# Weight and feature remainders on VectorE in place of GpSimd, in a hybrid diffusion layer

## Chip, core and metric

The kernel runs on one core of a Trainium2 chip. The metric is the device time of one execution in microseconds (us). Engines are named as the profile names them: PE is TensorE's matmul, PEld its weight load, DVE is VectorE, ACT is ScalarE, POOL is GpSimd, and SP is SyncE, which issues most DMAs. Each engine works off its own instructions strictly in their order, and waits on semaphores for what other engines and DMAs produce.

## The reference, cut to what matters

One layer of a backbone runs over 128 context tokens and 1024 latent tokens, with a width of 1024. In the kernel's order:

```python
h  = rmsnorm(x, norm1_w) * (1 + sc1) + sh1          # adaLN modulation
aq, ak, av, mq, mk, mv, mo, mg = split(h @ w_in)    # 2832 columns
attn_o = attention(aq, [ak, cached], [av, cached])  # 8 query heads, 2 key heads, 64 wide
hm     = bidirectional mLSTM(mq, mk, mv, gates)     # 4 heads, 128 wide, chunks of 128
x  = x + g1 * (concat(attn_o, hm * sigmoid(mo)) @ w_out)
h2 = rmsnorm(x, norm2_w) * (1 + sc2) + sh2
g, u = split(h2 @ w_gu)                             # 2 x 2816 columns
x  = x + g2 * ((silu(g) * u) @ w_down)
y  = rmsnorm(x, final_norm_w)
```

Everything is float32 outside, and the kernel keeps that accuracy. It splits an operand into an upper half, rounded to the type that the matmul reads (fp32r, or float16), and a lower half, the remainder `full - hi`. A product is then three matmuls: upper by upper, upper by lower, lower by upper. The lower halves are what this change is about.

## The kernel before, in words

The tokens stand in nine blocks of 128, and these in three chunks of 384 (`CB` = 3 blocks).

The work has these stages. First come the modulation vectors from `w_ada`, the norm of x, and `features(c)`, which makes the modulated features of a chunk as float16 pairs `hTh` and `hTl`. For each of eight column groups it writes the upper half on ACT and the full value on DVE, and subtracts (line 137, `sub`). The groups with an even number subtract on DVE, the others on POOL. Then the projections by `w_in` run: keys, values and gates, then q, then four mLSTM heads. Their weights are `Scaled` objects of four tiles each. `pairs()` makes float16 pairs of them. With its default `dve_every=2`, tiles 0 and 2 are done by one ACT instruction and one fused DVE instruction (line 222), and tiles 1 and 3 by two on ACT and a `sub` on POOL (line 226, shown as line 137). The pairs of keys, values and gates use `dve_every=1` and so the fused form alone. Attention and the mLSTM scans run woven between these matmuls.

`attn_out_first` and `prefill` apply `w_out`, and `norm2` makes the input of the FFN. Then the three FFN chunks follow (`gate_up`, `down`, `down_last`). A chunk works through 22 blocks of the FFN's width in five groups. For each block `gate_up` loads a piece of the gate columns and one of the up columns and runs 24 matmuls of 384 columns for each piece (lines 1315 to 1317). The activation follows: tanh on ACT (line 1333), two instructions on DVE into the tile tn (1334 and 1335), its upper half hl on ACT (1338), its lower half on POOL (also line 137, `hl<-tn,hl`, not touched by the change). After a group's four or five blocks `down` multiplies by `w_down` (lines 1115 to 1117) and adds into x on DVE (`add_gated`, lines 1104 and 1105). During the first two chunks the attention of the next chunk is woven in: scores S on PE (1035), row maximum st on DVE (1037), exp on ACT (1038), upper part ph on ACT (1041), lower part pl on DVE (1042), then two transposing DMAs and the products by the values (1059, 1060). S has one buffer.

All float32 weights, 216 pieces of `w_out`, `w_gu` and `w_down` in the buffers named raw, whi and wlo and a few more in borrowed buffers (`ir`, `ip`), go through `load_piece`. SP loads 512 KB into raw (two buffers), ACT copies it rounded into whi (line 154), and `sub` writes `raw - whi` to wlo (line 137). whi and wlo have five buffers each, so a piece can be prepared while PE works on earlier ones; a raw buffer is free again once its subtraction is done. A count decides the engine: every third piece subtracts on DVE, the two others on POOL.

The source gives priorities (`hot`) and interleavings (`weave`, `beside`). The final order of each engine's instructions is laid out ahead of time by the planner of the framework, which plays the program through with its own costs (`schedule_with_timeline_sim`). A change of an instruction's engine therefore changes the order that it plans.

Of the kernel before, what the change touches and what calls it, by code (L numbers as in the profile page):

```python
# [8 lines left out]
F32 = mybir.dt.float32  # L9
# [36 lines left out]
def hybrid_step(ctx: ExitStack, tc: tile.TileContext, I: dict, O: dict):  # L46
# [3 lines left out]
    dve = nc.vector  # L50
    pool = nc.gpsimd
# [6 lines left out]
    def nm(s):  # L58
        uid[0] += 1
        return f"{s}_{uid[0]}"  # L60
# [75 lines left out]
    def sub(out, full, hi, eng):  # L136
        (dve if eng == "dve" else pool).tensor_tensor(out=out, in0=full, in1=hi, op=ALU.subtract)  # L137

    lo_count = [0]

    def load_piece(srcs, shape, dve_every=3, raw=None, own=None):

        a, b = shape
        n = a * b

        def view(t):
            return t[:, :n].rearrange("p (a b) -> p a b", b=b)

        raw = raw or wp.tile([P, 1024], F32, name=nm("raw"), tag="raw", bufs=2)
        hi = own[0] if own else wp.tile([P, 1024], F32R, name=nm("whi"), tag="whi", bufs=5)  # L150
        lo = own[1] if own else wp.tile([P, 1024], F32R, name=nm("wlo"), tag="wlo", bufs=5)
        for part, ap_ in srcs:
            dma(part(view(raw)), ap_)
        nc.scalar.copy(hi[:, :n], raw[:, :n])  # L154
        lo_count[0] += 1
        sub(lo[:, :n], raw[:, :n], hi[:, :n].bitcast(F32), "dve" if lo_count[0] % dve_every == 0 else "pool")
        return view(hi), view(lo)

    full_view = lambda v: v
# [22 lines left out]
    class Scaled:  # L182
# [31 lines left out]
        def pairs(self, dve_every=2):  # L214
            out = []
            n, b = self.n, self.shape[1]
            for j, raw in enumerate(self.raws):
                w = wp.tile([P, 2, 1024], F16, name=nm("ipair"), tag="ipair", bufs=4)
                hi, lo = w[:, 0, :n], w[:, 1, :n]
                if j % dve_every == 0:  # L220
                    act(hi, raw[:, :n], AF.Copy, scale=self.scale)
                    dve.scalar_tensor_tensor(out=lo, in0=raw[:, :n], scalar=self.scale, in1=hi, op0=ALU.mult, op1=ALU.subtract)  # L222
                else:
                    act(raw[:, :n], raw[:, :n], AF.Copy, scale=self.scale)
                    nc.scalar.copy(hi, raw[:, :n])
                    sub(lo, raw[:, :n], hi, "pool")
                out.append(tuple(v.rearrange("p (a b) -> p a b", b=b) for v in (hi, lo)))
            return out

# [271 lines left out]
    def features(c):  # L501

        v = x3[c].rearrange("p b (k x) -> p k b x", k=KD)
        hh, hl = (t[c].rearrange("p k (b x) -> p k b x", b=CB) for t in (hTh, hTl))
        for k in range(KD):
            full = p0.tile([P, CB, P], F32, name=nm("full"), tag="full", bufs=4)
            for i, n in ((0, 1), (1, 2)) if c == 0 else ((0, CB),):
                cnd = 0 if n == 1 else 1
                s, t = scale1[:, k, cnd : cnd + 1], shift1[:, k, cnd : cnd + 1]
                act(hh[:, k, i : i + n], v[:, k, i : i + n], AF.Identity, scale=s, bias=t)  # L510
                dve.tensor_scalar(out=full[:, i : i + n], in0=v[:, k, i : i + n], scalar1=s, scalar2=t, op0=ALU.mult, op1=ALU.add)
            sub(hl[:, k], full, hh[:, k], "dve" if k % 2 == 0 else "pool")

    for c in range(NCH):
        with hot(100):
            features(c)
        prods = linear_tok(kvg_pairs, 0, 272, evac_kvg, (tuple(range(c * CB, c * CB + CB)),), bank if c == 1 else bankA)
        if c > 0:
            weave(prods, chain(steps, ada), KD, 10)
        else:  # L520
            emit(prods)
        if c == 0:
            normalise(2)
        if c == 1:
            turn(2)
# [597 lines left out]
    def out_pieces(half, own=None):  # L1123
        ws = []
        for n in range(2):
            pieces = []
            for j in range(2):
                r0 = half * 512 + 2 * j * P
                rows = w_out[r0 : r0 + 2 * P, n * 512 : (n + 1) * 512].rearrange("(a p) n -> p a n", p=P)
                pieces.append(load_piece([(full_view, rows)], (2, 512), raw=own and own[2], own=own))  # L1130
                own = None
            ws.append(pieces)
        return ws
# [74 lines left out]
    def attn_out_first(oT, ready):  # L1208
# [16 lines left out]
        def out():  # L1225
            for n in range(2):
                cs = slice(n * 512, (n + 1) * 512)
                ws = []
                for j in range(2):
                    rows = w_out[2 * j * P : (2 * j + 2) * P, cs].rearrange("(a p) n -> p a n", p=P)  # L1230
                    ws.append(load_piece([(full_view, rows)], (2, 512), raw=ir[2], own=(ip[j], ir[j])))
                for cnd in range(2):
                    dma(gt[:, 2 * n + cnd], g_d[0, cnd : cnd + 1, cs].to_broadcast([P, 512]))
                yield
                for i in range(CB):
                    while i not in ready:
                        yield
                    th, tl = mx[:, i, 0:4], mx[:, i, 4:8]
                    if n == 0:
                        dma(x1[:, i], xrow(i))  # L1240
                        nc.scalar.copy(th, oT[i])
                        sub(tl, oT[i], th.bitcast(F32), "pool")
                        yield
                    ps = out_block([ws], 0, th, tl)
                    v = x1[:, i, cs]
                    dve.tensor_tensor(out=gt[:, 4], in0=ps, in1=gt[:, 2 * n + (i > 0)], op=ALU.mult)
                    pool.tensor_tensor(out=v, in0=v, in1=gt[:, 4], op=ALU.add)
                    yield
                    if n == 1:
                        dma(x1a_d[i], x1[:, i])  # L1250
# [68 lines left out]
    def gate_up(a, f0, nf):  # L1319
        th, tl = a["h2"]  # L1320
        acts = a["act"] = []
        for f in range(f0, f0 + nf):
            if True:
                pg, pu = bank(), bank()
                for off, ps in ((0, pg), (D_FF, pu)):
                    src = w_gu[:, off + f * P : off + (f + 1) * P].rearrange("(k p) n -> p k n", p=P)
                    wh, wl = load_piece([(full_view, src)], (KD, P))
                    products(ps[:, 0:CT], wh, wl, th, tl)
                    yield 6
                parts = [(slice(0, CT), pg[:, 0:CT], pu[:, 0:CT])]  # L1330
            tn = fp.tile([P, CT], F32, name=nm("tn"), tag="tn", bufs=2)
            for cs, g, u in parts:
                act(tn[:, cs], g, AF.Tanh, scale=0.5)
                dve.scalar_tensor_tensor(out=tn[:, cs], in0=tn[:, cs], scalar=1.0, in1=u, op0=ALU.add, op1=ALU.mult)  # L1334
                dve.tensor_tensor(out=tn[:, cs], in0=tn[:, cs], in1=g, op=ALU.mult)
            hl = hlp.tile([P, 2, CT], F32R, name=nm("hl"), tag="hl", bufs=5)
            ah, al = hl[:, 0], hl[:, 1]
            nc.scalar.copy(ah, tn)  # L1338
            sub(al, tn, ah.bitcast(F32), "pool")
            acts.append((ah, al))  # L1340
# [207 lines left out]
```

## Time and profile before

| | |
|---|---|
| median of three runs | 1601.01 us (1599.53 to 1605.31) |
| the profiled execution | 1606.1 us, its span 1604.4 us |
| mean granted TensorE clock | 0.973 |
| busy: PE, PEld | 1502.1 us (94%), 1252.0 us (78%) |
| busy: DVE, ACT, POOL | 929.7 us (58%), 767.1 us (48%), 658.9 us (41%) |
| wlo on POOL, on DVE | 144 in 349.6 us, 72 in 87.2 us |

The span runs from the first to the last instruction. Busy time is the time in which an engine worked on at least one instruction; the end of a matmul is modelled, so that matmuls overlap in the records. In a group's row stand the source line, the engine, the operation, the tile written and those read, shapes, the count, then busy time and the mean of one, then the engine's idle time ahead of them and what ended it. Line 137 is the helper `sub`, so its rows are told apart by their tiles.

### The profile page before, as it was taken

What the parts mean: (1) busy time and instruction counts of PE and PEld (TensorE: products, weight loads), DVE (VectorE), ACT (ScalarE), POOL (GpSimd) and SP (SyncE); (2) the same over time, 40 slices, a digit from 0 to 9 for tenths busy, and PEclk for the clock granted to TensorE, in tenths of its full rate; (3) what the DMA queues carried; (4) which work ended last, traced back from release to release, by engine and by line L of the source; (5) the groups of instructions that cost most, each with busy time, mean ns of one, the idle gap of its engine ahead of it and who ended that gap; (6) DMA issues with size and microseconds to landing.
All of it is one profiled execution on the core that took longest, in us unless ns stands there. A gap on an engine that the chain in (4) does not pass through costs nothing. (4 is left out here: it accounts for less than half of the span.)

```text
span 1604.4 us, 23368 instructions
## 1 busy us (share of the span) xinstructions
PE 1502.1 (94%) x8539; PEld 1252.0 (78%) x8539; DVE 929.7 (58%) x1856; ACT 767.1 (48%) x1409; POOL 658.9 (41%) x526
## 2 busy tenths in 40 slices
PE   6888989899988779999999999999999999999996
PEld 3544557676766567989999989899898989899995
DVE  4778545745747575567443556777764474332445
ACT  4844455856655354535432444555562453333322
POOL 0243532333343443544444444443444445544443
PEclk9899999899999899999999999999999999999998
DMA  9474323442555736867653456887674455544442
GB/s 359 155 198 153 95 53 42 102 77 51 83 138 159 250 106 145 210 173 184 164 153 127 141 151 211 197 179 178 153 177 129 128 151 165 153 128 146 144 128 70
DMA packets 387880, 236.91 MB, mean 148 GB/s; under 512 B 170198, under 2 KB 346790, under 8 KB 387766
## 3 DMA queue, kind: packets, MB, share of 16 engines
q1 hardware_dynamic: 385110, 231.84, 53.7%
q10 hardware_dynamic: 2656, 3.58, 1.0%
q8 instruction: 67, 1.10, 0.3%
q14 instruction: 47, 0.39, 0.1%
HBM read 183.79 MB, written 13.26 MB: 123 GB/s over the span
## 5 line engine op out<-in xcount | busy, mean ns | idle before, releaser
L137 POOL TENSOR_TENSOR wlo<-raw,whi 128x1024 fp32r<-128x1024 f32 (+1 forms) x144 | 349.6, 2431 | 418.3 <-ACT whi L154 392.1
L154 ACT CAST whi<-raw 128x1024 fp32r<-128x1024 f32 (+1 forms) x216 | 221.6, 1026 | 386.3 <-DMA raw<-in_w_gu_dram 136.5
L1316 PE MATMUL mm<-aTl,whi 128*128 128x384 f32 x1056 | 355.1, 336 | 0.0
L1315 PE MATMUL mm<-aTh,whi 128*128 128x384 f32 x1056 | 354.1, 337 | 0.9 <-DVE tn L1334 0.9
L1317 PE MATMUL mm<-aTh,wlo 128*128 128x384 f32 x1056 | 354.7, 336 | 0.0
L1315 PEld LDWEIGHTS mm<-aTh,whi 128*128 128x128 f32 x1056 | 198.2, 188 | 2.2 <-DVE tn L1334 1.5
L1316 PEld LDWEIGHTS mm<-aTl,whi 128*128 128x128 f32 x1056 | 198.4, 188 | 0.8 <-DVE aTl L137 0.2
L1317 PEld LDWEIGHTS mm<-aTh,wlo 128*128 128x128 f32 x1056 | 198.4, 188 | 0.1
L137 DVE TENSOR_TENSOR wlo<-raw,whi 128x1024 fp32r<-128x1024 f32 (+1 forms) x72 | 87.2, 1211 | 150.8 <-ACT whi L154 150.8
L1115 PE MATMUL mm<-whi,hl 128*128 128x512 f32 x372 | 144.9, 393 | 2.7 <-ACT hl L1338 1.4
L1116 PE MATMUL mm<-wlo,hl 128*128 128x512 f32 x372 | 145.7, 393 | 0.0
L1117 PE MATMUL mm<-whi,hl 128*128 128x512 f32 x372 | 142.9, 392 | 1.3 <-POOL hl L137 1.3
L486 PE MATMUL wi<-ipair,hT 128*128 128x384 f16 (+2 forms) x408 | 138.7, 341 | 2.6 <-DVE G L499 1.2
L1042 DVE SCALAR_TENSOR_TENSOR pl<-pr,st,ph 128x1152 f16<-128x1152 f32 (+1 forms) x72 | 107.3, 1491 | 55.6 <-ACT ph L1041 50.7
L487 PE MATMUL wi<-ipair,hT 128*128 128x384 f16 (+2 forms) x408 | 138.2, 339 | 1.3 <-DVE ipair L222 1.3
L488 PE MATMUL wi<-ipair,hT 128*128 128x384 f16 (+2 forms) x408 | 136.5, 340 | 1.7 <-DVE hT L137 1.7
L137 POOL TENSOR_TENSOR hl<-tn,hl 128x384 fp32r<-128x384 f32 x66 | 86.0, 1303 | 98.5 <-ACT hl L1338 98.3
L1038 ACT ACTIVATE pr<-S,st 128x1152 f32<-128x1152 f32 (+1 forms) x72 | 81.5, 1131 | 77.8 <-DVE st L1037 67.5
L1105 DVE TENSOR_TENSOR x<-x,t 128x512 f32<-128x512 f32 x102 | 117.4, 1173 | 0.8
L1334 DVE SCALAR_TENSOR_TENSOR tn<-tn,mm 128x384 f32<-128x384 f32 x66 | 36.4, 551 | 139.7 <-PE mm L1317 97.7
L1037 DVE TENSOR_REDUCE st<-S 128x1 f32<-128x1152 f32 (+1 forms) x72 | 88.8, 1233 | 25.8 <-PE S L1035 25.3
L1035 PE MATMUL S<-kst,qT 128*128 128x384 f32 (+1 forms) x400 | 88.8, 351 | 5.4 <-ACT pr L1038 5.3
(369 smaller groups left out, 2712.9 us busy)
## 6 DMA issues: line engine op xcount, KB each, us to landing
raw<-in_w_gu_dram SPq DMA_DIRECT2D x132, 512.0 KB
raw<-in_w_down_dram SPq DMA_DIRECT2D x60, 512.0 KB
a<-in_w_ada_dram SPq DMA_DIRECT2D x24, 512.0 KB
gl<-g_d SPq DMA_DIRECT2D x36, 256.0 KB
aw<-in_w_ada_dram SPq DMA_DIRECT2D x16, 512.0 KB
iraw<-in_w_in_dram SPq DMA_DIRECT2D x32, 256.0 KB
raw<-in_w_out_dram SPq DMA_DIRECT2D x12, 512.0 KB
x<-in_x_sample_dram SPq DMA_DIRECT2D x11, 512.0 KB
```

Of the source, the lines that this page charges most:

```text
L137: (dve if eng == "dve" else pool).tensor_tensor(out=out, in0=full, in1=hi, op=ALU.subtract)
L154: nc.scalar.copy(hi[:, :n], raw[:, :n])
L486: mm(ps[:, :n], ah, wh[:, k % 2, c0 : c0 + n], start=(k == 0), stop=False)
L487: mm(ps[:, :n], ah, wl[:, k % 2, c0 : c0 + n], start=False, stop=False)
L488: mm(ps[:, :n], al, wh[:, k % 2, c0 : c0 + n], start=False, stop=(k == KD - 1))
L1105: eng.tensor_tensor(out=x1[:, cs], in0=x1[:, cs], in1=t, op=ALU.add)
L1115: mm(ps, ah, wh[:, k % 2, :], start=(k == 0), stop=False)
L1116: mm(ps, ah, wl[:, k % 2, :], start=False, stop=False)
L1117: mm(ps, al, wh[:, k % 2, :], start=False, stop=(k == nk - 1))
L1315: mm(ps, wh[:, k, :], th[:, k, :], start=(k == 0), stop=False)
L1316: mm(ps, wh[:, k, :], tl[:, k, :], start=False, stop=False)
L1317: mm(ps, wl[:, k, :], th[:, k, :], start=False, stop=(k == KD - 1))
```

## The change

Three calls of `sub` that chose POOL, always or for a part of their calls, now choose DVE. They are the lower halves of the split weights in `load_piece` (and with them the counter and its parameter go), the lower halves of the tiles 1 and 3 in `pairs()`, and those of the odd column groups in `features`. The arithmetic, the buffers and their counts, the loads, and all other work on POOL, among it the lower halves of the activations (`hl`), stay.

```diff
-    lo_count = [0]
-
-    def load_piece(srcs, shape, dve_every=3, raw=None, own=None):
+    def load_piece(srcs, shape, raw=None, own=None):
...
         nc.scalar.copy(hi[:, :n], raw[:, :n])
-        lo_count[0] += 1
-        sub(lo[:, :n], raw[:, :n], hi[:, :n].bitcast(F32), "dve" if lo_count[0] % dve_every == 0 else "pool")
+        sub(lo[:, :n], raw[:, :n], hi[:, :n].bitcast(F32), "dve")
...
                     act(raw[:, :n], raw[:, :n], AF.Copy, scale=self.scale)
                     nc.scalar.copy(hi, raw[:, :n])
-                    sub(lo, raw[:, :n], hi, "pool")
+                    sub(lo, raw[:, :n], hi, "dve")
...
-            sub(hl[:, k], full, hh[:, k], "dve" if k % 2 == 0 else "pool")
+            sub(hl[:, k], full, hh[:, k], "dve")
```

## The prediction, made before the change was run

> **What bounds the kernel now.** I read the page's busy shares first, then the windows view with five stages and the attention stretch of the second FFN chunk.
>
> ```profile
> PE 1502.1 (94%) x8539; PEld 1252.0 (78%) x8539; DVE 929.7 (58%) x1856; ACT 767.1 (48%) x1409; POOL 658.9 (41%) x526
> ...
> 160.00:480.00 320.00, 299.62 (x1909) 210.53 (x1906) 178.80 (x456) 190.77 (x531) 122.14 (x224) 0.96 0.40 80
> 480.00:640.00 160.00, 129.93 (x674) 99.94 (x675) 106.03 (x260) 77.71 (x151) 61.74 (x49) 0.90 0.60 164
> 640.00:1560.00 920.00, 913.34 (x4976) 843.18 (x4975) 506.99 (x705) 396.74 (x521) 417.29 (x203) 1.00 0.59 160
> ...
> 1000.00:1200.00 200.00, 196.83 (x1129) 179.93 (x1128) 143.71 (x196) 115.99 (x150) 83.22 (x38) 1.00 0.76 178
> ...
> 1442.10:1475.30 33.20, 33.20 (x193) 33.20 (x192) 10.37 (x13) 11.30 (x15) 17.62 (x9) 1.00 0.51 151
> ```
>
> Columns: stretch, length, busy time and count of PE, PEld, DVE, ACT, POOL, then granted clock, DMA share, GB/s. The three FFN chunks fill 640 to 1560 us, and there PE is idle for 920.00 - 913.34 = 6.7 us. PE busy is modelled, so I check it by the count: in 1442.10 to 1475.30, gate and up products alone, 193 matmuls start in 33.20 us, one every 172 ns, with a weight load busy all the time at clock 1.00. Nothing done to the subtractions can quicken that stream; it can only be starved. DVE is at 55% there and POOL at 45%, averages over many short waits. Before 640 us PE has real holes (30.1 us of idle in 480 to 640 alone).
>
> What ends PE's idle time, in the view of waits (who, for whom: total us, times, longest), first for PE in 620 to 1560 us, then for PE and PEld before 620 us:
>
> ```profile
> PE mm L1115 <- ACT hl L1338: 1.4, 2, 1.1
> PE mm L1117 <- POOL hl L137: 1.3, 2, 0.8
> ...
> PE mm L1115 <- DVE tn L1334: 1.1, 1, 1.1
> ...
> PE mm L1315 <- DVE tn L1334: 0.9, 2, 0.4
> ...
> PE S L1035 <- ACT pr L1038: 0.5, 1, 0.5
> ```
>
> ```profile
> PE mm L1148 <- POOL wlo L137: 1.9, 1, 1.9
> ...
> PEld mm L1149 <- DVE mx L137: 2.1, 2, 1.3
> ...
> PEld L488 <- DVE hT L137: 2.2, 1, 2.2
> ...
> PEld L813 <- POOL ipair L137: 0.2, 1, 0.2
> ```
>
> In the FFN PE waits on the handover of a group's last activation (tn on DVE, hl on ACT and POOL) for 4.7 us in all, and not once on a weight's lower half. Before it, one wait of 1.9 us is for a moved subtraction and one of 2.2 us for a feature's.
>
> **The change part by part.** It moves three kinds of subtraction from POOL to DVE. These rows (duration min/median/max in ns) give their price on either engine, and those of the neighbours; the first of them are from the tile view of wlo, hl, hT and ipair, then L1105 by source, then groups from the page and the group view:
>
> ```profile
> L137 POOL TENSOR_TENSOR wlo<-raw,whi x144: 1290/2402/4175, 546.3 to 1574.2; 128x1024 fp32r<-128x1024 f32 x138, 128x512 fp32r<-128x512 f32 x6
> L137 DVE TENSOR_TENSOR wlo<-raw,whi x72: 684/1225/2161, 547.6 to 1570.5; 128x1024 fp32r<-128x1024 f32 x66, 128x512 fp32r<-128x512 f32 x6
> L137 POOL TENSOR_TENSOR hl<-tn,hl x66: 992/1026/2139, 656.6 to 1576.7; 128x384 fp32r<-128x384 f32 x66
> L137 POOL TENSOR_TENSOR hT<-full,hT x12: 912/919/2154, 48.3 to 83.9; 128x384 f16<-128x384 f32 x12
> L137 DVE TENSOR_TENSOR hT<-full,hT x12: 534/546/900, 49.6 to 84.1; 128x384 f16<-128x384 f32 x12
> L222 DVE SCALAR_TENSOR_TENSOR ipair<-iraw,isc,ipair x10: 1276/1348/2999, 87.1 to 391.1; 128x1024 f16<-128x1024 f32 x10
> L137 POOL TENSOR_TENSOR ipair<-iraw,ipair x10: 2122/2128/3103, 89.6 to 392.9; 128x1024 f16<-128x1024 f32 x10
> L137 POOL TENSOR_TENSOR ir<-ir,ip x3: 2344/2356/2362, 469.2 to 519.6; 128x1024 fp32r<-128x1024 f32 x3
> L1105 DVE TENSOR_TENSOR x<-x,t x102: 673/686/2887, 693.0 to 1594.9; 128x512 f32<-128x512 f32 x102
> ...
> L1105 DVE TENSOR_TENSOR x<-x,t 128x512 f32<-128x512 f32 x102 | 117.4, 1173 | 0.8
> ```
>
> DVE gains 138 wlo x 1.225 + 6 x 0.684 = 173.2 us, 3 ir (wlo in borrowed buffers) x 1.225 = 3.7, 10 ipair at L222's minimum 1.276 = 12.8, and 12 hT x 0.546 = 6.6: together 196 us. It also gets something back. L1105, two SBUF inputs, has a median of 686 ns but a mean of 1173 ns. Two timelines (start, duration, engine, line) show why: two of them took 4.13 us while POOL ran two wlo.
>
> ```profile
> 1079.03 4.13 DVE L1105 TENSOR_TENSOR x<-x,t 128x512 f32<-128x512 f32 x2
> ...
> 1076.88 5.72 POOL L137 TENSOR_TENSOR wlo<-raw,whi 128x1024 fp32r<-128x1024 f32 x2 [5.09 <-issue]
> ```
>
> So (1.173 - 0.686) x 102 = 49.7 us of DVE are time lost to POOL, and I take all of it as returned (POOL's remaining hl could keep some). DVE's net gain is about 147 us: 929.7 becomes 1077 of 1604, 67%. Where it is fullest, 1000 to 1200 us, these rows count what moves and what comes back (POOL's wlo, then DVE's L1105 there):
>
> ```profile
> 1000.00:1200.00 200.00, 65.74 (x26) 1.00 0.76 178
> ...
> 1000.00:1200.00 200.00, 20.10 (x18) 1.00 0.76 178
> ```
>
> 143.7 + 26 x 1.225 - (20.10 - 18 x 0.686) = 167.8 of 200 us, 84%. DVE fits, but its queue is in order, and that is the question.
>
> The Trainium skill ("SBUF — State Buffer", Who interferes with whom) says that a VectorE instruction with two SBUF inputs and a GpSimd instruction that reads SBUF block each other, the later one for the whole of the earlier. The 4.13 us above agree with it.
>
> What a moved subtraction waits for and holds up is in the whole view of waits, with SyncE's own queue behind it:
>
> ```profile
> POOL wlo L137 <- ACT whi L154: 392.1, 114, 10.0
> DVE wlo L137 <- ACT whi L154: 150.8, 41, 9.3
> ACT whi L154 <- DMA raw<-in_w_gu_dram: 136.5, 58, 5.8
> ...
> POOL hl L137 <- ACT hl L1338: 98.3, 29, 7.2
> DVE tn L1334 <- PE mm L1317: 97.7, 30, 7.5
> ...
> ACT pr L1038 <- DVE st L1037: 67.5, 39, 6.2
> ...
> SPq L153 <- POOL wlo L137: 294.4, 110, 5.8
> SPq L153 <- DVE wlo L137: 125.5, 55, 8.0
> ```
>
> A sub on POOL that waits for its upper half stops nobody but POOL and the hl behind it (mean 392.1 / 114 = 3.4 us). On DVE the same wait stands ahead of tn, of the PSUM additions L1104 and L1105, and of attention's row maximum st, for which ACT's exp and then PE's S wait. But ACT itself stands at that cast meanwhile, for at most 5.8 us where it waits for gate and up weights, and tn's tanh comes behind it on ACT. The sub issues no DMA; the next raw load on SyncE waits until it is done, so the load starts 2.402 - 1.225 = 1.18 us earlier where DVE is free, later where it is not.
>
> The terms, each on PE's path:
> - Features (hT): PE's 2.2 us stall at the first chunk. Without POOL beside it DVE loses less (0.900 us at most against 0.546, that is 0.35 us), but does four more subs. Bounds -2.2 to +6.6 (all twelve exposed); I take -0.5, nearest the stall's own row.
> - Pairs (ipair): PE waited 0.2 us for them, so the gain ends there; the loss ends at 12.8 us, all ten on DVE exposed. DVE is 178.80 / 320 = 56% busy in that stage; I take +1.
> - w_out pieces (ir, and prefill's wlo): PE waited 1.9 us on POOL and 2.1 us on mx, which stood behind a wlo on DVE that took 2.16 us; each halves: -2. Bounds -4.0 to +8.6 (seven subs at 1.225 exposed).
>
> ```profile
> 547.60 2.16 DVE L137 TENSOR_TENSOR wlo<-raw,whi 128x1024 fp32r<-128x1024 f32 x1 [2.41 <-ACT whi L154]
> 549.68 0.68 DVE L137 TENSOR_TENSOR mx<-mm,mx 128x512 fp32r<-128x512 f32 x1
> ```
>
> - FFN handover, relief: hl no longer queues behind a 2.4 us wlo on POOL. Of 4.7 us I take a third, -1.5; at most -4.7.
> - FFN handover, delay: at the fifteen ends of a gate-up group a sub can stand between PE's last product and tn. All of them: 15 x 1.225 = 18.4 us; none: 0. DVE now carries 72 of 216 pieces and waits on tn and hl cost 3.4 us (1.4 + 1.1 + 0.9); at three times the pieces, three times that, so +6.8 more. I take +5, since a queue with its order replanned avoids part.
> - Attention: 0.5 us of S waiting now, three times that: +1; at most 48 heads x 1.225 = 59 us, at least -0.5.
>
> Sum: -0.5 + 1 - 2 - 1.5 + 5 + 1 = +3.0 us. The profiled execution took 1606.1 us with a span of 1604.4; the change makes it 1609.1. The median of the three runs, 1601.0, lies 5.1 us below the profiled one, so I forecast 1604.0.
>
> The Trainium skill ("Perfetto Trace Analysis", Optimizing Scalar/DVE Operations) says that offloading VectorE to GpSimd may make sense where VectorE is saturated, and may not help since they share a port. By its first half the move is wrong in 1000 to 1200 us; at 84% the rows stop short of that.
>
> **The rivals.**
> - Slower by the queue: DVE stands at subs whose upper half is late, ahead of tn, at every group end: +18.4 us, 1619. For it: the waits of 9.3 us. Against: 72 subs are there already and PE is idle 6.7 us in 920. It decides once 7 of 15 ends are hit (8 us).
> - Slower by hl held: every DVE sub beside an hl makes it 2.139 instead of 1.026 us; at fifteen ends 15 x 1.113 = 16.7 us, 1618. For it: the spread of hl's own row. Against: hl today meets POOL's own wlo instead. The Trainium skill ("SBUF — State Buffer", Who interferes with whom) is where such a hold would come from.
> - Slower before the FFN: pairs and w_out pieces fully exposed, 12.8 + 8.6 = 21.4 us, 1622. Against: DVE has room in both stages.
> - Faster: every stall with a moved sub in it goes, 2.2 + 0.2 + 4.0 + 4.7 = 11.1 us, 1590. For it: L1105's contention and 294.4 us of SyncE's waits for POOL. Against: PE, saturated, did not feel either.
> - No shorter on DVE: the subs take 2.161, their maximum, if POOL still gets in the way. Then DVE in 1000 to 1200 holds 167.8 + 26 x 0.936 = 192 us, and the first rival follows.
>
> **How the numbers follow.** About 0.5% (8 us) is what a measurement of this kernel can tell from no change: 1593 to 1609. Forecast 0.55; queue 0.16, with the last rival in it; hl held 0.06; front 0.06; faster 0.17. Hence faster 0.17, same 0.55, slower 0.28. The forecast's own range is 1597 to 1609. Both signs matter, so the range reaches from the faster case, 1590, to the worst of the slower ones, 1622; the attention bound, +59, is left out.
>
> **What would show it.** In the changed profile: no wlo, ipair, hT or ir on POOL, POOL near 659 - 385 = 274 us (144 x 2.402 + 3 x 2.356 + 10 x 2.128 + 12 x 0.919 = 385), DVE near 1077, L1105's mean near 0.69. PE idle in the FFN stretch of 10 to 12 us, with tn as releaser, would prove the delay term; over 20 us the queue rival; under 4 us the faster one. S waiting for pr by more than 3 us would refute the attention term, and a shorter stretch up to 640 us the front terms. Wrong would also be a replanned order that moves work between the stages at all.

## The result, and the profile after

The changed kernel takes 1589.74 us (median, 1585.16 to 1592.12), against 1601.55 us for the kernel before beside it: a ratio of 0.992, 95% interval 0.9891 to 0.9949. It was measured again in a later series at 1589.54 us, ratio 0.9914 (0.9895 to 0.9932). It is faster by 0.8%; forecast was 1604.0 us. The profiled execution took 1592.1 us, with a span of 1590.3. The profiled execution of the kernel before (1606.1 us) lies 5 us above its median, the one of the kernel after 2 us above, so what follows compares single executions.

Lines behind the edits move up by one to three: L1315 becomes L1312, L811 L808, L1105 L1102, L1038 L1035. First the page's busy line of the kernel after:

```profile
PE 1494.7 (94%) x8539; PEld 1249.4 (79%) x8539; DVE 1027.2 (65%) x2025; ACT 768.8 (48%) x1409; POOL 267.4 (17%) x357
```

POOL fell about as forecast (274 us). DVE grew by 98 us, not by 147. The windows view (stretch, length, busy of PE, PEld, DVE, ACT, POOL, clock, DMA share, GB/s), first of the kernel before, for two stretches that the prediction did not show, then of the kernel after:

```profile
160.00:420.00 260.00, 243.21 (x1520) 168.57 (x1518) 147.73 (x380) 154.40 (x421) 94.07 (x169) 0.95 0.36 72
640.00:1550.00 910.00, 903.34 (x4918) 833.18 (x4917) 505.90 (x704) 393.62 (x517) 411.56 (x200) 1.00 0.59 160
```

```profile
160.00:420.00 260.00, 244.86 (x1543) 172.43 (x1544) 154.42 (x417) 160.64 (x438) 80.46 (x168) 0.96 0.35 77
640.00:1550.00 910.00, 905.06 (x4950) 838.74 (x4949) 593.25 (x843) 400.17 (x525) 83.12 (x64) 1.00 0.60 161
...
1000.00:1200.00 200.00, 200.00 (x1171) 185.38 (x1170) 156.57 (x218) 113.27 (x150) 13.73 (x12) 1.00 0.78 175
```

In both stretches PE starts more matmuls in the same time, 23 and 32 more. The windows are fixed in time, so they do not hold quite the same work. How much was won in which stage is read better from two lines of PE that run once through a stage: the products of the four mLSTM heads (L811) and the gate and up products (L1315). Their rows give duration, then the first and the last start. Before, then after:

```profile
L811 PE MATMUL wi<-hT,ipair x96: 323/326/524, 169.8 to 412.6; 128*128 128x384 f16 x96
L1315 PE MATMUL mm<-aTh,whi x1056: 331/334/440, 642.1 to 1574.2; 128*128 128x384 f32 x176
```

```profile
L808 PE MATMUL wi<-hT,ipair x96: 323/326/527, 168.8 to 404.1; 128*128 128x384 f16 x96
L1312 PE MATMUL mm<-aTh,whi x1056: 331/334/423, 632.9 to 1560.2; 128*128 128x384 f32 x176
```

The span shrank by 14.1 us: 1.0 up to the first head product, 7.5 in the heads (242.8 to 235.3 us), 0.7 from there to the FFN, 4.8 in the FFN (932.1 to 927.3), 0.1 behind it. I call these two lengths the heads' stage and the FFN stage from here on. The end of the heads is uncertain by 2 us: after, the last product of the line behind (L809) starts 2.3 us later than the last of L808, before only 0.1 us later. Measured to that line, the heads gain 5.3 us and the stretch behind them 2.9.

The price of the moved work, and of its neighbours (tile view, then the group's row of L1102):

```profile
L137 DVE TENSOR_TENSOR wlo<-raw,whi x216: 680/1224/2040, 539.9 to 1557.7; 128x1024 fp32r<-128x1024 f32 x102, 128x512 fp32r<-128x512 f32 x6
L137 POOL TENSOR_TENSOR hl<-tn,hl x66: 1007/1332/1846, 647.8 to 1562.8; 128x384 fp32r<-128x384 f32 x66
```

```profile
L1102 DVE TENSOR_TENSOR x<-x,t 128x512 f32<-128x512 f32 x102 | 71.0, 707 | 0.9
```

A piece takes 1.224 us on DVE, as before. x's addition takes 707 ns instead of 1173. hl on POOL is slower, 1.33 instead of 1.03 us at the median. PE's waits after, in the FFN with its edges (620 to 1546 us), and the waits of the two queues in question over the whole span:

```profile
PE mm L1313 <- DVE aTl L137: 2.7, 2, 1.6
PE po L1057 <- DMA plT<-pl: 1.3, 1, 1.3
PE mm L1144 <- DVE t L1195: 1.2, 1, 1.2
PE mm L1146 <- DVE mx L137: 1.1, 1, 1.1
PE S L1032 <- ACT pr L1035: 1.0, 1, 1.0
```

```profile
DVE wlo L137 <- ACT whi L152: 203.2, 102, 4.7
...
DVE tn L1331 <- PE mm L1314: 64.7, 40, 2.9
```

No row with tn or hl as the releaser is left; the handover of a group's last activation, 4.7 us before, costs PE nothing now. The waits on mx and t stood there before too (1.1 and 0.9 us), but those on aTl (2.7) and most of plT's (0.5 before) are new. Net, PE's waits in 640 to 1550 us fall from 6.7 to 5.0 us; the rest of the FFN stage's 4.8 us stands in no row of waits.

### The profile page after: what moved, and what is told of

Its sections match the earlier page's. It is cut to its first block, busy times and chain, and to the rows that moved or that the text cites. A ratio compares the mean times of both kernels' runs of the same rounds, so it can differ in the third digit from the quotient of the medians.

```text
span 1590.3 us, 23425 instructions
## 1 busy us (share of the span) xinstructions
PE 1494.7 (94%) x8539; PEld 1249.4 (79%) x8539; DVE 1027.2 (65%) x2025; ACT 768.8 (48%) x1409; POOL 267.4 (17%) x357
## 4 chain that ended last, share of the span: by engine, by line
PE 75%; DVE 9%; DMA 8%; ACT 4%; issue 2%; SPq 1%; POOL 1%; ACTq 0%; DVEq 0%; POOLq 0%
PE mm L1313 11%; PE mm L1314 11%; PE mm L1312 11%; PE mm L1112 5%; PE mm L1113 5%; PE mm L1114 5%; PE S L1032 4%; PE wi L485 3%; PE wi L483 3%; PE wi L484 3%; PE mm L1144 1%; PE mm L1145 1%; DMA aw<-in_w_ada_dram 1%; PE po L1057 1%; PE po L1056 1%
## 5 line engine op out<-in xcount | busy, mean ns | idle before, releaser
L137 DVE TENSOR_TENSOR wlo<-raw,whi 128x1024 fp32r<-128x1024 f32 (+1 forms) x216 | 260.5, 1206 | 203.8 <-ACT whi L152 203.2
L1312 PE MATMUL mm<-aTh,whi 128*128 128x384 f32 x1056 | 353.2, 336 | 0.0
L1312 PEld LDWEIGHTS mm<-aTh,whi 128*128 128x128 f32 x1056 | 198.1, 188 | 0.6
L483 PE MATMUL wi<-ipair,hT 128*128 128x384 f16 (+2 forms) x408 | 136.2, 337 | 1.8 <-ACT hT L507 1.2
L484 PE MATMUL wi<-ipair,hT 128*128 128x384 f16 (+2 forms) x408 | 136.4, 337 | 0.0
L485 PE MATMUL wi<-ipair,hT 128*128 128x384 f16 (+2 forms) x408 | 132.5, 337 | 1.0 <-DVE hT L137 1.0
L1039 DVE SCALAR_TENSOR_TENSOR pl<-pr,st,ph 128x1152 f16<-128x1152 f32 (+1 forms) x72 | 93.8, 1303 | 33.8 <-ACT ph L1038 33.7
L1034 DVE TENSOR_REDUCE st<-S 128x1 f32<-128x1152 f32 (+1 forms) x72 | 88.9, 1235 | 14.6 <-PE S L1032 14.1
L1035 ACT ACTIVATE pr<-S,st 128x1152 f32<-128x1152 f32 (+1 forms) x72 | 81.3, 1129 | 29.6 <-DVE st L1034 25.6
L1038 ACT ACTIVATE ph<-pr,st 128x1152 f16<-128x1152 f32 (+1 forms) x72 | 83.8, 1165 | 23.2 <-DVE st L1037 6.7
L1101 DVE TENSOR_TENSOR t<-mm,gl 128x512 f32<-128x512 f32 x102 | 68.9, 685 | 28.1 <-DMA gl<-g_d 10.2
L1032 PEld LDWEIGHTS S<-kst,qT 128*128 128x128 f32 x400 | 70.6, 191 | 14.7 <-ACT pr L1035 7.0
```

The source lines that it names most:

```text
L483: mm(ps[:, :n], ah, wh[:, k % 2, c0 : c0 + n], start=(k == 0), stop=False)
L484: mm(ps[:, :n], ah, wl[:, k % 2, c0 : c0 + n], start=False, stop=False)
L485: mm(ps[:, :n], al, wh[:, k % 2, c0 : c0 + n], start=False, stop=(k == KD - 1))
L1032: mm(S[:, n, 0:w], qT[:, h, :], kst[kv][:, t, c0 + n * w : c0 + (n + 1) * w], start=(t == 0), stop=(t == 1))
L1312: mm(ps, wh[:, k, :], th[:, k, :], start=(k == 0), stop=False)
```

## The experiments

### One part at a time

Theory: the gain comes from the pieces in the FFN and from the pairs in the heads' stage, both because POOL's subtractions had held DVE. Rival: it comes from one part, or from the order planned anew. Each kernel has one or two of the three moves.

Pieces alone (`load_piece` as in the change; pairs and features as before):

```diff
-        sub(lo[:, :n], raw[:, :n], hi[:, :n].bitcast(F32), "dve" if lo_count[0] % dve_every == 0 else "pool")
+        sub(lo[:, :n], raw[:, :n], hi[:, :n].bitcast(F32), "dve")
```

> The changed kernel with features and pairs back on POOL: only the weight pieces (wlo, and the three ir) subtract on DVE. In the profiles the first gate-up product came 9.2 us earlier after the change (642.1 to 632.9 us), and the rest of the FFN gained another 4.8 us. If the pieces carry the FFN's part and the features and pairs carry the front's: 1594 to 1597 us, first gate-up product near 642 us, PE idle after it as in the changed kernel. If the front's gain comes from the pieces too (w_out's, through POOL and SyncE): 1588 to 1591 us. If it is only a lucky new order: any time from 1585 to 1610, with no relation between the parts.

Features and pairs, pieces as before:

```diff
-                    sub(lo, raw[:, :n], hi, "pool")
+                    sub(lo, raw[:, :n], hi, "dve")
...
-            sub(hl[:, k], full, hh[:, k], "dve" if k % 2 == 0 else "pool")
+            sub(hl[:, k], full, hh[:, k], "dve")
```

> The kernel before with only features and pairs (22 subtractions) moved to DVE; the pieces as before. If these carry the front's gain: first gate-up product near 633 us, 1593 to 1596 us. If the front's gain came with the pieces: 1600 to 1603 us. My prediction had +0.5 us for these two terms together: 1602 us.

Features alone (the second of these two edits), and pairs alone (the first):

> The kernel before with only the twelve feature subtractions moved to DVE. If the front's 6 us come from the features (the first stall, and the half-clock time behind it): 1594 to 1596 us. If they come from the pairs: 1599 to 1601 us. My prediction had -0.5 us.

> The kernel before with only the ten subtractions of the pairs moved to DVE. In the trace of before, a POOL subtraction of a pair held a DVE instruction of the scan (2.23 us in place of 0.35) and the fused one (3.00 in place of 1.28), and PE waited behind them at the change of heads. If that holding is the cause: 1593 to 1596 us, and the PE stalls at the changes of heads shorter. If not: 1599 to 1602 us. My prediction had +1 us.

The change once more, beside the two:

> The changed kernel once more, beside the others on one chip: 1588 to 1592 us. Pieces alone gave -2.7 us and features with pairs -5.9 us: if the two parts add up, -8.6 us, 1591; if they help each other, 1587 to 1589 us.

And the combination that these point to, pairs and pieces without the features:

> Pairs and weight pieces on DVE, features left as they were. Theory (the change is a sum of a gain of the pairs, a gain of the pieces and a loss of the features): pairs alone brought 1586.4, and pieces shorten the FFN by 5 to 7 us, so 1579 to 1582, FFN from the first gate-up product to down_last near 927, and S's and the strips' stalls of 156 to 176 us as short as with the pairs alone. Rival (the parts take the same stalls away and do not add): about the time of the pairs alone, 1585 to 1588. Rival (a replanned order decides, not the parts): anything from 1579 to 1592, the front not like that of the pairs alone.

Measured, with the two stages from the same two lines of each kernel's trace:

| on DVE | median us | ratio to before (95%) | heads us | FFN us |
|---|---|---|---|---|
| as before | 1599.9 to 1601.6 | 1 | 242.8 | 932.1 |
| features | 1605.47 | 1.0020 (1.0009 to 1.0031) | 243.1 | 930.6 |
| pairs | 1586.37 | 0.9898 (0.9882 to 0.9914) | 230.7 | 933.1 |
| features, pairs | 1594.00 | 0.9968 (0.9952 to 0.9984) | 232.3 | 931.6 |
| pieces | 1597.18 | 0.9980 (0.9967 to 0.9993) | 238.2 | 925.3 |
| pairs, pieces | 1582.42 | 0.9878 (0.9857 to 0.9899) | 230.4 | 925.9 |
| all three (the change) | 1589.74, 1589.54 | 0.9920, 0.9914 | 235.3, 236.2 | 927.3, 925.1 |

Each ratio is good to about 2 or 3 us, and a difference of two to 3 or 4. By differences of ratios times 1601 us, the pairs bring 16.3 us alone, 16.3 beside the pieces, 8.3 beside the features. The pieces bring 3.2 us alone and 3.2 beside the pairs (7.7 to 8.6 beside both others; the second is within the noise), although the FFN stage is shorter by 5 to 8 us wherever they are on DVE and nowhere else. The features cost 3.2 us alone, 11.2 beside the pairs, 5.8 to 6.7 beside both. Pairs and pieces without features make the fastest version of the study, faster than the kernel before and, by the medians, 7 us faster than the change.

### Why the pairs gain

PE waited 0.2 us for a pair before. But this is PE's view of waits in 160 to 420 us, kernel before, first four of eleven rows (16.9 us in all):

```profile
PE S L1035 <- ACT pr L1038: 4.9, 1, 4.9
PE wi L811 <- DVE QT L657: 2.4, 1, 2.4
PE mm L873 <- DVE nu L876: 2.3, 1, 2.3
PE mm L866 <- ACT kT L770: 2.1, 2, 1.5
...
```

And with the pairs alone on DVE, first three of six rows (7.3 us in all):

```profile
PE wi L811 <- DVE QT L657: 2.8, 1, 2.8
PE mm L866 <- ACT kT L770: 2.1, 2, 1.5
PE mm L116 <- ACT it L869: 1.0, 1, 1.0
...
```

S's wait for the softmax (4.9 us), nu (2.3) and th (1.9) are gone: nothing that the change touches is named in these rows. What stood behind nu is seen in the timeline of before (start, duration, engine, line):

```profile
301.95 2.20 POOL L137 TENSOR_TENSOR ipair<-iraw,ipair 128x1024 f16<-128x1024 f32 x1 [4.64 <-ACT ipair L225]
302.07 2.23 DVE L887 SCALAR_TENSOR_TENSOR hm<-nu,dn,hm 128x128 f32<-128x128 f32 x1
...
306.61 2.13 POOL L137 TENSOR_TENSOR ipair<-iraw,ipair 128x1024 f16<-128x1024 f32 x1
306.82 3.00 DVE L222 SCALAR_TENSOR_TENSOR ipair<-iraw,isc,ipair 128x1024 f16<-128x1024 f32 x1
309.74 0.41 DVE L876 TENSOR_TENSOR nu<-mm,it 128x258 f32<-128x258 f32 x1
```

hm, 0.352 us at its median, lasts until POOL has finished its pair; the fused lower half, 1.348 at its median, lasts 3.00. All that is queued on DVE behind them is late, nu among it, for which PE waits from 308.0 to 310.3 us. th's 1.9 us goes back in part to the same cause: at 393.17 us dn (L881) takes 1.85 us on DVE beside a POOL pair, 0.14 at its shortest, and hm, so and th come behind it in turn. The Trainium skill ("SBUF — State Buffer", Who interferes with whom) says that a VectorE instruction with two SBUF inputs contends with a GpSimd instruction that reads SBUF; these lines agree, and hm's excess of 1.9 us is their measure of it.

A hole on PE costs more than itself. The windows of before around S's wait:

```profile
202.30:207.60 5.30, 0.41 (x4) 0.04 (x1) 0.06 (x1) 0.46 (x2) 0.00 (x0) 0.87 0.25 4
207.60:212.80 5.20, 5.20 (x18) 2.94 (x19) 2.21 (x13) 2.50 (x10) 1.66 (x5) 0.50 0.09 19
```

After 4.9 us of idle PE runs 5.2 us at clock 0.50, so another 2.6 us are lost. The Trainium skill ("TensorE: Matmul & The Clock Gate", Part 1: The HAM clock gate) says that half the clock is granted after an idle window of about 3.4 us, and the full one after a busy window; the trace agrees with the drop, and here the half clock lasted longer than one such window.

But this largest wait is not DVE held by a pair: in 202.30 to 207.60 us DVE works 0.06 us and POOL not at all. The exp that S waits for stood on ACT behind ACT's load of the queries (qr), and that load waits until SP's write of them (q_d) has landed. SP's queue and ACT's exp, kernel before, then pairs alone:

```profile
195.97 0.42 SPq L804 DMA_DIRECT2D out_new_state_n_dram<-cs  x1
196.69 0.80 SPq L732 DMA_DIRECT2D q_d<-qraw  x2
...
207.05 0.37 ACT L1038 ACTIVATE pr<-S,st 128x128 f32<-128x128 f32 x1 [9.15 <-DMA q_d<-qraw]
```

```profile
191.19 0.80 SPq L732 DMA_DIRECT2D q_d<-qraw  x2
192.04 0.44 SPq L804 DMA_DIRECT2D out_new_state_n_dram<-cs  x1
...
193.97 0.37 ACT L1038 ACTIVATE pr<-S,st 128x128 f32<-128x128 f32 x1 [1.84 <-DMA q_d<-qraw]
```

With a small write of the state (0.5 KB) issued ahead of the queries, the exp starts 10.4 us after their issue; with the queries first, 2.8 us. In the eighteen traces S waits here, 2.8 to 4.9 us, in the seven kernels that issue such a 0.5 KB write (L804) just ahead of the queries, and in none of the eleven others. So S's 4.9 us, and the half clock behind them, go with the order of SP's queue, which the planner lays out. No run changed that order alone, and why the small write delays the large one was not tested. It is not all of the gain: neither the features alone nor features and pairs have this wait, and there the pairs still bring 8.3 us.

Two explanations of the pairs' gain remain: POOL no longer holds DVE, or a pair is simply ready earlier. To part them, the pairs go to DVE, and POOL repeats the subtraction into a spent tile that nobody reads:

```diff
-                    sub(lo, raw[:, :n], hi, "pool")
+                    sub(lo, raw[:, :n], hi, "dve"); sub(raw[:, :n], raw[:, :n], hi, "pool")
```

> The kernel before with the pairs' ten subtractions on DVE, and behind each of them a subtraction on POOL of the same size and the same two inputs, whose result nobody reads (it overwrites the spent raw tile). The products no longer wait for POOL, but POOL still runs. Theory (POOL holds DVE's two-input operations, hm and the fused lower half among them): the gain is lost, 1597 to 1603, stage of the four heads back from 209 to 216 us or more, hm or the fused lower half stretched to over 2 us again. Rival (the pair was late because POOL is slow, 2.1 against 1.3 us): the gain stays, 1585 to 1589, stage near 209.

Measured: 1596.01 us, ratio 0.9972 (0.9956 to 0.9988), heads' stage 237.9 us. Its tile rows of the pairs, behind those of the kernel with the pairs alone on DVE:

```profile
L222 DVE SCALAR_TENSOR_TENSOR ipair<-iraw,isc,ipair x10: 1267/1281/1418, 86.2 to 373.4; 128x1024 f16<-128x1024 f32 x10
L137 DVE TENSOR_TENSOR ipair<-iraw,ipair x10: 1200/1226/1760, 88.2 to 375.2; 128x1024 f16<-128x1024 f32 x10
```

```profile
L222 DVE SCALAR_TENSOR_TENSOR ipair<-iraw,isc,ipair x10: 1273/1285/3054, 83.6 to 381.4; 128x1024 f16<-128x1024 f32 x10
L137 DVE TENSOR_TENSOR ipair<-iraw,ipair x10: 1212/1221/1918, 85.6 to 383.8; 128x1024 f16<-128x1024 f32 x10
L137 POOL TENSOR_TENSOR iraw<-iraw,ipair x10: 2123/2132/3235, 86.9 to 386.3; 128x1024 f32<-128x1024 f32 x10
```

Nobody reads POOL's result, and yet (0.9972 - 0.9898) x 1601 = 11.8 of the 16.3 us are gone; the fused half lasts up to 3.05 us again, and PE's waits in 160 to 420 us come to 14.6 us, 2.8 of them S's, 2.6 on sd and 1.4 on nu, both DVE's. That is 1 us short of the range that the theory gave, and 7 above the rival's. So a pair that is ready earlier does not by itself keep the gain. But the shadow also keeps a raw tile longer and changes the order (S's 2.8 us are back, and a 0.5 KB state write again stands ahead of the queries), so how much of the 11.8 us is DVE held by POOL stays open.

Whether the second ACT pass of the pairs lies on the path was tried in the fastest version, with the fused form for all four tiles (`pairs(self, dve_every=1)`):

> Pairs and pieces on DVE, and all pairs in the fused form (one ACT pass and one DVE instruction; the second ACT pass of 1024 columns of tiles 1 and 3 goes). If ACT's pass lies on the path of the heads: 1577 to 1581, the stage of the four heads under 209 us. If not: 1581 to 1584, or a shift of 2 to 5 us to either side by the new order alone.

Measured: 1586.70 us, ratio 0.9913 (0.9896 to 0.9930), heads' stage 235.6 us. It lost 5.6 us with less work to do: S waits 4.5 us for the softmax again, with a 0.5 KB state write ahead of the queries. The pass was not on the path; the order is the likely reason.

### Why the pieces gain

Three rivals: POOL's pieces hold DVE; hl stands behind a piece in POOL's queue; the order. In the first test POOL works again, beside pieces that DVE has finished: it adds a zero column to two of three wlo, in place. PE waits for these as well.

```diff
+        if own is None:
+            lo_count[0] += 1
+            if lo_count[0] % 3:
+                pool.tensor_tensor(out=lo[:, :n], in0=lo[:, :n].bitcast(F32), in1=zcol.to_broadcast([P, n]), op=ALU.add)
```

> The changed kernel, and for two of three pieces POOL afterwards adds a column of zeros to the finished wlo in place: about 2.4 us of SBUF reading on POOL each, as before the change, the subtraction itself still on DVE. If the gain in the FFN comes from POOL being out of the way (DVE instructions held, hl behind long POOL work), it goes: L1105's mean back to 1.0 us or more, FFN stalls back by 4 to 7 us, 1594 to 1597 us. If it comes from the shorter subtraction and the earlier load of raw: 1589 to 1591 us.

Measured: 1601.29 us, ratio 1.0005 (0.9991 to 1.0019); the gain is gone, and more than the theory gave. It is no clean test of held DVE, though: the addition takes 1.9 us on POOL and not 2.4, x's addition has a mean of 0.80 us and not of 1.0 or more, PE waits 1.8 us for POOL's result, and no wait on tn or hl is back. In the second test only hl moves to DVE, pieces as before:

```diff
-sub(al, tn, ah.bitcast(F32), "pool")
+sub(al, tn, ah.bitcast(F32), "dve")
```

> The kernel before with one edit: the activations' lower half hl (66 of them) subtracts on DVE, everything else as before, so that POOL's wlo stay and DVE is still held by them. If the FFN's gain is that hl no longer queues on POOL behind a wlo: the waits on hl and tn go and the FFN gains 4 to 7 us, 1594 to 1598 us. If it is DVE being held by POOL: 1600 to 1604 us, since DVE gets 66 more instructions to be held.

Measured: 1606.68 us, ratio 1.0040 (1.0023 to 1.0057), slower than either side gave. PE's waits on tn and hl in 620 to 1560 us fall from 4.7 to 1.7 us, but S's rise from 0.5 to 2.4 and those for the transposing DMAs from 0.5 to 3.2. And the dose: every piece on POOL.

> The kernel before with every weight piece's subtraction on POOL, none on DVE (216 in place of 144). Theory (POOL's pieces hold DVE's two-input operations and hl): the FFN grows, from 932.6 us by 3 to 8, and the 512-column products' stalls from 8 us upward; 1603 to 1610. Rival (the gain of the pieces on DVE came from the order or from sparing POOL's latency in the group ends only): FFN within 2 us of before, 1599 to 1603.

Measured: 1630.02 us, ratio 1.0183 (1.0158 to 1.0207), far more than either side expected. The gate and up line (L1315, or its number there) in two kernels, the shadow and all on POOL:

```profile
L1320 PE MATMUL mm<-aTh,whi x1056: 333/334/532, 633.1 to 1571.7; 128*128 128x384 f32 x176
```

```profile
L1315 PE MATMUL mm<-aTh,whi x1056: 331/334/689, 649.2 to 1599.7; 128*128 128x384 f32 x176
```

The FFN stage lasts 938.6 and 950.5 us, against 933.2 with hl on DVE, 925.3 with the pieces alone on DVE and 925.9 in the fastest kernel. By dose it is 926 us with no piece on POOL, 932 with two thirds there, 950 with all; in the eighteen traces of the study, kernels with no POOL work on pieces lie between 925.1 and 927.3, those with two thirds between 930.6 and 933.4. This stage, unlike the front, hardly moves with the order. So POOL's work on pieces costs the FFN its time, but by which way is only partly seen. Taking hl off POOL does not bring the gain, so hl's place behind a piece is not all of it. The seven waits of the handover before have several causes, by the timeline of that trace: 0.9 us follow a final-norm operation (L1365) that takes 2.9 us instead of 0.74 beside a piece on POOL, 0.8 an hl queued behind a piece on POOL, 0.5 an hl stretched to 1.84 us, 1.1 a piece that DVE itself subtracts ahead of tn, and 1.4 a late cast on ACT. With all on POOL, PE's waits name the handover again, and the softmax (620 to 1560 us):

```profile
PE mm L1315 <- DVE tn L1334: 5.7, 2, 2.9
PE S L1035 <- ACT pr L1038: 4.5, 4, 2.5
```

The half clock adds to that: the mean granted clock in 640 to 1550 us is 0.99 there, and 1.00 before.

The shadow lost more than the handover (938.6 against 932.1 us). In its trace the 512-column products of `down` and `w_out` start every 234 ns at the median, against 227 after; a tile that moves all later addresses by 4 bytes came with it. So the tile was made 128 bytes wide, and in another kernel the address was moved by 4 bytes without any shadow:

```diff
-    zcol = cp.tile([P, 1], F32, name="zcol")
+    zcol = cp.tile([P, 32], F32, name="zcol")[:, 0:1]
```

> The shadow kernel again (POOL adds a column of zeros to two of three finished wlo), with that column in a tile of 128 bytes instead of 4. With 4 bytes, all tiles behind it moved by 4 bytes, and the 512-column matmuls of down started every 234 ns instead of 227. If the address did that: 227 ns again, some 6 us faster than with 4 bytes, 1593 to 1597 us, and what is left over the changed kernel (3 to 6 us) is POOL's doing. If POOL's reading did it: 234 ns and 1600 to 1603 us again.

```diff
-    vsc = cp.tile([P, 4], F32, name="vsc")
+    vsc = cp.tile([P, 5], F32, name="vsc")[:, 0:4]
```

> The whole change with one small tile widened by 4 bytes, so that all tiles allocated after it move by 4 bytes as they do in the shadow kernel; no shadow operation. If the address sets the interval of the 512-column products: 232 to 234 ns between their starts, FFN near 935 us, 1597 to 1601. If POOL's reads of wlo set it: 226 to 227 ns, FFN 925.6 to 927.8, 1588 to 1592.

Measured: the wide tile 1602.99 us, ratio 1.0006 (0.9994 to 1.0018), 232 ns; the moved address 1585.60 us, ratio 0.9906 (0.9883 to 0.9930), 227 ns, below either range that was given. An address shift of 4 bytes is not the cause. The 512-column line of `down` (L1115 before) in the first shadow and with the moved address:

```profile
L1120 PE MATMUL mm<-whi,hl x372: 388/396/484, 679.6 to 1538.2; 128*128 128x512 f32 x186
```

```profile
L1112 PE MATMUL mm<-whi,hl x372: 387/389/481, 671.9 to 1521.1; 128*128 128x512 f32 x186
```

It is 7 ns a product (5 with the wide tile), with the shadow alone, and not while POOL subtracts as in the kernel before (389 ns there too). Why was not settled. Over the 1116 products of `down`'s three lines 7 ns make 7.8 us, by estimate most of the 11.3 us by which the shadow's FFN stage exceeds that of the changed kernel.

### Why the features cost

Theory A: DVE has too much to do. Theory B: the new order. First the halves of the features are swapped, odd on DVE and even on POOL, which moves no work to either engine (`k % 2 == 1`), on the kernel before and on the fastest version:

> The kernel before with the features' even groups on POOL and the odd ones on DVE, so the same twelve subtractions on either engine. It measures what a new order alone does. Theory (features on DVE cost 4.6 us because DVE carries more): no change, ratio 1.000 within 0.001, and PE's stalls between 155 and 176 us like before's. Rival (the order that the planner lays out decides): a shift of 2 to 5 us to either side, with the strip product placed ahead of the first head again or not.

> Pairs and pieces on DVE, features' even groups on POOL and odd ones on DVE, the same number on either. Theory B (order): a shift of 2 to 5 us to either side of 1582.4; the swap alone brought -3.4 us on the kernel before. Theory A (DVE's load): no change, 1581 to 1584.

Then all of them on POOL, on the fastest version, which takes twelve off DVE:

> Pairs and pieces on DVE as in the best version so far (1582.4, span 1575.0), and all 24 subtractions of the features on POOL, none on DVE. Theory A (the features cost time on DVE because DVE is full there): with 12 fewer on DVE the kernel gains, 1575 to 1582. Theory B (the new order costs, PE stalls of 4 to 6 us at the modulation row's product near 160 us and at S near 175 us): it loses like the whole change, 1585 to 1592, with those stalls, although DVE does less. Rival C: POOL's 0.9 us subtractions hold the fused and two-input operations at 48 to 84 us and shift everything by up to 12 x 0.9 = 11 us, seen as a later start of the keys', values' and gates' products.

Measured: the swap makes the kernel before 1597.32 us, ratio 0.9976 (0.9961 to 0.9991), and the fastest version 1590.24 us, ratio 0.9936 (0.9916 to 0.9955). The same edit without a change of load brings 3.8 us in one place and costs 9.3 in the other (7.8 by the medians), the second more than the 2 to 5 us that were expected. Part of both is S's wait for the softmax from above: the first kernel is without it, the second has 4.3 us of it. With all on POOL it is 1582.07 us, ratio 0.9891 (0.9872 to 0.9910): twelve fewer on DVE bring nothing. B's 1585 to 1592 did not come either, though the stall on part that it named did. So nothing supports theory A, and a new order alone is worth as much as the whole effect. PE's waits in 150 to 205 us, of the changed kernel, of the one with the features alone, and of all features on POOL:

```profile
PE S L1032 <- DVE qT L137: 4.1, 1, 4.1
PE mm L347 <- ACT part L441: 3.8, 1, 3.8
...
```

```profile
PE S L1035 <- DVE qT L137: 5.8, 1, 5.8
PE mm L350 <- ACT part L444: 5.1, 1, 5.1
...
```

```profile
PE mm L350 <- ACT part L444: 3.3, 1, 3.3
PE mm L788 <- POOL wv L786: 0.6, 1, 0.6
PE S L1035 <- DVE qT L137: 0.5, 1, 0.5
...
```

Kernels before and the fastest have one row there, 2.4 and 2.6 us on QT. In PE's list of matmuls, the last strip product of the modulation row (L344) and the product that reads its part (L350) stand 18 entries apart before and in the fastest kernel, 4 in the changed kernel and with the features alone, and 8 with all on POOL: with 4 and 8 PE reaches L350 before ACT's part is ready. With the halves swapped they stand 10 apart, and PE does not wait. But neither wait explains the times: the kernel with all features on POOL has the one on part and is not slower, and the swap on the kernel before has S waiting 5.0 us for qT and is faster. No kernel was run with the features on DVE and the old order, so B stands on the swap and on these rows, is not shown for the features themselves, and which step of the order costs most stays open.

## Why the prediction was wrong, point by point

The sign of the whole was wrong. By stages: the sum said +3.0 us, the two profiled executions differ by -14.1 us of span (the medians by -11.8).

- **Features, -0.5 (bounds -2.2 to +6.6).** Measured +3.2 to +11.2. The stall that it reckoned with shrank by 0.7 us, from 2.2 to 1.5 (waits of PEld after, below), much as the term said. But the term looked for exposure of the subtractions only, and the new stalls, on part and qT, came 100 us later, most likely by a new order.

```profile
PEld L485 <- DVE hT L137: 1.5, 1, 1.5
```

- **Pairs, +1 (bounds -0.2 to +12.8).** The main failure. Measured -8.3 to -16.3. The failed step is "PE waited 0.2 us for them, so the gain ends there": it took the waits that name the moved tile as the whole of what the moved instruction costs. The instruction also holds DVE, and that cost is booked under other names: the wait on nu (2.3 us) goes back to DVE held by a pair, and the one on th (1.9) in part. Another 4.9 us, S's wait on pr, went with the order of SP's queue, and the half clock behind the holes came on top. How the 16.3 us divide between holding and order stays open; without S's wait on either side the pairs bring 8.3. The prediction had priced just this for L1105, as busy time given back, and did not carry it to the waits of PE; the page's rows for hm (maximum 2.229 us) and L222 (2.999) were the hint.
- **w_out pieces, -2.** The two waits shrank as the term said, and a little more: PE's 1.9 us on POOL's wlo became 0.8 on DVE's, and PEld's 2.1 on mx became 0.2 (470 to 620 us after), -3.0 us. The stretch is not shorter by as much (0.7 or 2.9 us, see above), since others grew: PE's wait on hm_d from 4.2 to 6.4 us, S's on pr to 3.5.
- **FFN handover, relief, -1.5 (at most -4.7).** Its bound came true, all 4.7 us. The third that I took was a guess without a row. But 2.7 us on aTl are new, which no term had. And of the 3.4 us that the next term lays to DVE's pieces, only 1.1 followed a piece on DVE.
- **FFN handover, delay, +5.** Did not occur. The step "at three times the pieces, three times that" fails: on the whole trace DVE's waits on whi went from 150.8 us in 41 (longest 9.3) to 203.2 us in 102 (longest 4.7), so a third more, and shorter ones; DVE's waits for the last product ahead of tn fell from 97.7 to 64.7 us. POOL's 392.1 us of waiting for whi did not move to DVE.
- **Attention, +1.** S waits 1.0 us in the FFN instead of 0.5, and a transposed lower part 1.3 instead of 0.5. About right, and under the 3 us that would have refuted it.
- **Busy times.** POOL 267.4 against 274 and the piece's 1.225 us were right. DVE was forecast at 1077 and has 1027.2; in 1000 to 1200 us 156.57 against 167.8. Of the 196 us moved, not 50 but 98 came back: besides x's addition (L1105), the lower part of the softmax gave 12 us (L1042 from 102.9 to 91.0 us), and hm, the final norm and others the rest.
- **Rivals.** "Slower by the queue", "slower before the FFN" and "no shorter on DVE" are refuted by the rows above. "hl held" happened in kind: hl's median is 1.332 instead of 1.026 us, 0.3 us more instead of the 1.1 that was priced, and PE does not wait for it. "Faster" gave 1590 and was right in size, with 0.17 of the chance, but not in content: of its 11.1 us the handover (4.7), 3.0 of the 4.0 for w_out and 0.7 of the 2.2 for the features went as it said, but other waits grew in the same stretches, and the largest part of the gain, 7.5 us in the heads (5.3 by the later line), is none of its terms. So its 1590 was in part luck. The argument against it, that PE "did not feel" L1105's contention, was wrong: PE felt such contention in the heads' stage (nu and th), where it is not saturated, and for 0.9 us in the FFN. "Wrong would also be a replanned order" was the right warning, with no price beside it; the swap gives one, up to 9 us.

## What to carry to other kernels

An instruction that holds another engine shows up in PE's waits under the name of whatever was queued behind the held one: when a move takes POOL away from DVE, list every DVE operation that lasts far above its median while POOL runs, and follow who waited for those. Then look up each large wait by its time: the largest one of the heads, named for a softmax, belonged to a DMA's place in a queue. Repeating a moved operation with a result that nobody reads helps to price an engine's mere presence, as long as the order stays; here it did not. Where a planner lays the order out anew, an edit that moves no work gives the size of what order alone does, here up to 9 us, and any smaller effect in such a stage means little; a stage that stayed the same under every order (here the FFN) can be read to 1 or 2 us.

## What was unexpected of the hardware

Half of the moved busy time, 98 of 196 us, was given back to DVE by operations that kept their work. The cost of POOL's pieces rises steeper than their number: 0, 144 and 216 pieces there make an FFN stage of 926, 932 and 950 us, the last with more half clock. The queries' write, issued just behind a 0.5 KB write on SP's queue, let the exp that stood behind it start 10.4 us after the issue, and 2.8 us when issued ahead of it. And the shadow's in-place addition on POOL came with 512-column products that start every 232 to 234 ns instead of 227 on PE; the Trainium skill ("SBUF — State Buffer", Who interferes with whom) says that PE waits for no other engine's SBUF access, and the runs neither explain these 7 ns nor tie them to that access.
